# Leaving one weight tile of each light-expert chunk unsplit, as fp32, in a two-layer decoder trunk

## The chip, the cores and the metric

The kernel runs on one core of a Trainium2 chip. The metric is the device time of one launch in microseconds (us), here the median of three runs. TensorE (PE) multiplies, VectorE (DVE) and ScalarE (ACT) work on tiles in SBUF and PSUM, and SyncE (SP) issues the loads from HBM.

## The reference, cut to what matters

Two decoder layers on a sequence of 256 tokens of width 1024. Each mixes attention and a state-space scan; the first ends in a dense feed-forward block, the second in eight experts of which each token uses two. All inputs are float32. The experts are the part that the change touches:

```python
def _swiglu(h, wg, wu, wd):
    return (jax.nn.silu(h @ wg) * (h @ wu)) @ wd
...
    logits = (x2d @ w_router).astype(jnp.float32)
    top_v, top_i = lax.top_k(logits, TOP_K)
...
        return _swiglu(xb, wg[e], wu[e], wd[e]) * g[:, None]
```

Here wg and wu are 1024 x 3584 and wd is 3584 x 1024 for each of the eight experts.

## The kernel before

**Weights.** All weights come as tiles of 128 x 1024 float32 (512 KB), each by one DMA on SP's queue. An expert is worked through in 7 chunks (`NCH`) of 512 hidden columns, and a chunk has 12 tiles: 0 to 3 of the gate matrix, 4 to 7 of the up matrix, 8 to 11 of the down matrix. So an expert is 7 x 12 = 84 tiles or 44.04 MB.

**Splitting.** `load` (L510) fetches a tile `w` and hands it to `split` (L528): ACT writes a copy rounded to fp32r, `wh`, and DVE writes the rest, `wl` = `w` - `wh`, again as fp32r. PE multiplies by `wh` and `wl` in place of the float32 tile. `load` has an argument `whole` that leaves the split out and returns `(w, None)`; the mixer of the first layer uses it for its first eight weight tiles, whose matmuls stand in the trace as `bank<-w,h`.

**Heavy and light experts.** After routing, the experts are sorted by how many tokens they got. The four with most tokens are heavy: 128 rows each, activations split as well, three matmuls for each 128 x 512 piece of a weight tile (L545). The four others are light: at most 64 tokens each, the rounded activations in columns 0 to 63 of the stationary operand (`lx`, or `ht2` on the way down) and their rests in columns 64 to 127. A light expert needs only two matmuls for each piece, one by `wh` and one by `wl` (`both`, L1398); `join` (L1403) adds the lower half of the bank to the upper one. `light_up` (L1410) works tiles 0 to 7 of a chunk and writes `sg` and `ht2`, `light_down` (L1432) tiles 8 to 11. The places are taken in the order 0, 4, 1, 5, 2, 6, 3, 7 (`TURNS`), where 0 to 3 are heavy and 4 to 7 light, so a heavy expert and a light one follow each other and a light one comes last. In `moe` (L1442) the down half of a chunk is issued after the up half of the next.

**Order of the work.** Nothing is written to the engines directly. Every operation goes into a plan (`Plan.add`, L170) with its cost (`Plan.cost`, L209) and, on PE, its columns (`Plan.cols`, L204). `Plan.order` (L238) then sets one order of operations on all engines, each by the longest path that it still has before it, with corrections by stage (`BONUS`); the loads stay in the order in which the program asks for them. Tiles `w`, `wh`, `wl` and most others share 44 slots of 512 KB (`NM`), so a load can start only when a slot is free. `split` marks its ACT copy with a turn, so that splits start in the order of the loads, and with the number of `wh` that may be alive (`ks`).

Of the kernel before, what the change touches and what calls it, by code (L numbers as in the profile page):

```python
# [10 lines left out]
F32 = mybir.dt.float32  # L11
F32R = mybir.dt.float32r
# [16 lines left out]

TURNS = (0, 4, 1, 5, 2, 6, 3, 7)  # L30
GROUPS = {0: (0,), 1: (1,), 2: (2, 3), 4: LIGHT}
HEADS = [0, 4, 1, 5, 2, 6, 3, 7]
EPS = 1e-6
BIG = 1e30
# [113 lines left out]
class Plan:  # L148
# [54 lines left out]
    @staticmethod  # L203
    def cols(method, a):  # L204
        n, k = int(np.prod(a[2].shape[1:])), a[1].shape[0]
        return n * k / 128 * (2 if method == "transpose" else 1 if a[1].buf.dtype == F32R else 4)

    @staticmethod
    def cost(eng, method, a, k):  # L209
        size = lambda v: int(np.prod(v.shape[1:]))  # L210
        if method == "registers":
            return 0.5
        if eng == "DMA":
            return int(np.prod(a[0].shape)) * 4 / Plan.rate + 0.01
        n = max(size(v) for v in a if isinstance(v, View))
        if eng == "PE":
            if method == "transpose":
                return 2 * size(a[2]) / 2400 + 0.001
            if a[1].buf.dtype == F32R:
                return max(size(a[2]), 256) / 2400 + Plan.between  # L220
            return 4 * max(size(a[2]), size(a[1])) / 2400 + 0.0054
        if eng == "ACT":
            return 0.05 + n * 0.000876 + (0.06 if any(isinstance(v, View) for v in k.values()) else 0)
        if eng == "POOL":
            return max(0.35, 0.05 + n * 0.0006)
        if method in ("tensor_scalar", "tensor_copy"):
            fast = all(v.buf.kind != "ps" for v in a if isinstance(v, View))
            ptr = method == "tensor_scalar" and isinstance(a[2], View)
            return 0.066 + n * (0.00055 if fast else 0.00104) + 0.062 * ptr
        ptr = method in ("scalar_tensor_tensor", "tensor_scalar") and any(isinstance(v, View) for v in a[2:3])  # L230
        return 0.068 + n * 0.00104 + 0.062 * ptr
# [6 lines left out]
    def order(self, slots):  # L238
# [65 lines left out]
        while done < n:  # L304
# [83 lines left out]
            if e == "PE":  # L388
                if ticks.get(int(t / TICK) - 1, 0) < WARM:
                    cost *= 2  # L390
                m = int((t + cost) / TICK)
                ticks[m] = ticks.get(m, 0) + o["cols"]
# [53 lines left out]
class Kernel:  # L446
# [500 lines left out]
    def attention(self, l, prm, rs0, qb, kvb, whole):  # L947
# [63 lines left out]
        def score(gi):  # L1011
            t, h0, n = groups[gi]
            bank = self.bank()
            nk = 128 * (t + 1)
            for i in range(0, n, 2):
                self.mm3(bank[:, i * nk:(i + 2) * nk], *(x if x is None else x[:, (h0 + i) // 2, t, :] for x in qT),
                         *(x if x is None else x[:, :, 0:nk] for x in kd), True, True)
            mk = mask if t else mask[:, 128:256]
            st, pt[gi] = self.two("st")
            st = st.rearrange("p (h k) -> p h k", h=n)  # L1020
            tt(st, bank.rearrange("p (h k) -> p h k", h=n), mk.unsqueeze(1).to_broadcast([128, n, nk]), OP.add)
            c0 = 8 * t + h0
            cols = nm[:, c0:c0 + n]
            nc.vector.tensor_reduce(cols, st, AX.X, OP.max)
            stt(cols, cols, -1.0, nsink[:, h0:h0 + n], OP.mult, OP.min)
            for i in range(n):
                act(st[:, i, :], st[:, i, :], AF.Exp, bias=nm[:, c0 + i:c0 + i + 1], accum_out=den[:, c0 + i:c0 + i + 1])
            sc[gi] = st
# [369 lines left out]
    def both(self, out, x, w, first):  # L1398

        for i, b in enumerate(w):  # L1400
            self.nc.tensor.matmul(out, x, b, start=first and i == 0, stop=False, skip_group_check=True)

    def join(self, bank):  # L1403

# [5 lines left out]
    def light_up(self, src, of, rs):  # L1410
        g = []
        for q in range(2):
            bank = self.bank()
            for n in range(4):
                w = self.load(src[4 * q + n])
                for i in range(2):
                    self.both(bank, of(2 * n + i), [x[:, 512 * i:512 * i + 512] for x in w], n + i == 0)
            g.append(self.join(bank))
        h = self.H("sg")[0:ROOM]
        self.act(h, g[0], AF.Silu, scale=rs)  # L1420
        self.stt(h, g[1], rs, h, OP.mult, OP.mult)
        bank = self.bank()
        for i in range(4):
            self.nc.tensor.transpose(bank[:, ROOM * i:ROOM * i + ROOM], h[:, 128 * i:128 * i + 128], self.ident[0:ROOM, 0:ROOM])
        b = bank[:, :4 * ROOM].rearrange("p (k m) -> p k m", k=4)
        ht = self.H("ht2", F32R)
        v = ht.rearrange("p (k q m) -> p k q m", k=4, q=2)
        self.act(v[:, :, 0], b, AF.Copy)
        self.tt(v[:, :, 1], b, v[:, :, 0].bitcast(F32), OP.subtract)
        return ht  # L1430

    def light_down(self, i, src, ht, acc, then):  # L1432
        for half in range(2):
            for n in range(2):
                w = self.load(src[2 * half + n])
                for m in range(2):
                    k = 2 * n + m
                    self.both(acc[half], ht[:, 128 * k:128 * k + 128], [x[:, 512 * m:512 * m + 512] for x in w], i + k == 0)
            if then:
                then(half)  # L1440

    def moe(self, R):  # L1442
# [11 lines left out]
        for turn, j in enumerate(TURNS):  # L1454
            if j in GROUPS:
                self.plan.after = [mark] if j else []
                got = self.gather(GROUPS[j], hn) if j < HEAVY else self.gather_light(hn)
                self.plan.after = []
                for n, i in enumerate(GROUPS[j]):
                    rows[i] = (n, *got)  # L1460
# [210 lines left out]
def _lay_out(inp):  # L1671
# [4 lines left out]
    w = f(inp["w_in"])  # L1676
    q = w[:, :, :512].reshape(DEPTH, D, 8, 64)[:, :, HEADS].reshape(DEPTH, D, 512)
    kv, u = w[:, :, 512:768], w[:, :, 768:]
# [6 lines left out]

    both = lambda ms, ncol: np.stack([tiles(m, ncol) for m in ms])
    a["win_u"], a["win_q"], a["win_kv"] = both(u, 512), both(q, 512), both(kv, 256)
    a["wglu"] = both(f(inp["w_glu"]), 512)
    wo = f(inp["w_o"])
    wo = np.concatenate([wo[:, :512].reshape(DEPTH, 8, 64, D)[:, HEADS].reshape(DEPTH, 512, D), wo[:, 512:]], axis=1)  # L1690
    a["wo"] = both(wo, 512)

    def ffn(g, u, d):
# [18 lines left out]
    prm[:, :, 65] = np.tile(f(inp["k_norm_g"]), (1, 2))  # L1712
    prm[:, :, 66:74] = f(inp["sinks"])[:, None, HEADS]
    ag = f(inp["attn_out_g"]).reshape(DEPTH, 8, 64)[:, HEADS].reshape(DEPTH, 512)
    gains = [f(inp["attn_norm_g"]), np.concatenate([ag, f(inp["ssm_out_g"])], axis=1), f(inp["ffn_norm_g"])]
# [23 lines left out]
```

## Time and profile before

| | us |
|---|---|
| median of 3 runs | 1455.64 |
| lowest and highest | 1454.06 to 1456.81 |
| the profiled execution's own time | 1456.36 |
| its span | 1454.5 |
| PE matmul busy | 1395.2 (96%) |
| PE weight load busy | 1085.9 (75%) |
| DVE busy | 1239.1 (85%) |
| ACT busy | 1049.5 (72%) |
| bytes moved, mean rate | 422.59 MB, 291 GB/s |

The span is what the profile covers; the remaining 1.9 us of the profiled execution lie around it. The busy shares are means over the mixers, the dense block (up to about 480 us) and the experts (from then on), which have different limits, so the experts have to be read for themselves. All recorded operations stand at one line of a helper (L443), so they are told apart by their tiles.

### The profile page before, as it was taken

To read this page: it belongs to the slowest core of one execution; us is meant where nothing else is said; L and a number is where in the kernel's file an instruction comes from. 1 tells how busy PE (TensorE), PEld (TensorE's weight loads), DVE (VectorE), ACT (ScalarE), POOL (GpSimd) and SP (SyncE) were. 2 spreads that over 40 slices of the span, in tenths; PEclk is the share of its full clock that TensorE was granted. 3 is DMA by queue.
4 is the path that set the end of the run, shared out by engine and by line. 5 is a ranking of instruction groups with operands and counts; after the bars stand their busy time and mean duration, and the time that the engine had idled before them with its cause. 6 is when DMAs were issued, how large, how long until landed. Compare 5 with 4: busy or idle time off the path is not lost. (4 is left out here: it accounts for less than half of the span.)

```text
span 1454.5 us, 20913 instructions
## 1 busy us (share of the span) xinstructions
PE 1395.2 (96%) x6558; PEld 1085.9 (75%) x6558; DVE 1239.1 (85%) x1668; ACT 1049.5 (72%) x1350; POOL 25.4 (2%) x44
## 2 busy tenths in 40 slices
PE   7999999999999999997999998999999989999996
PEld 4888888888888777875678875668886667887564
DVE  7888885454795798998889999989999999999996
ACT  5586754445446488797787788978879878778875
POOL 3000110000000000000000000000000000000000
PEclk9999999999999999998999999989999999999998
DMA  5356155554347589599999999989999999999990
GB/s 215 106 175 230 66 167 183 189 192 173 121 171 283 199 302 348 193 395 340 348 375 380 384 400 367 393 326 362 386 383 381 348 397 390 380 384 393 387 378 33
DMA packets 116901, 422.59 MB, mean 291 GB/s; under 512 B 13360, under 2 KB 13872, under 8 KB 116784
## 3 DMA queue, kind: packets, MB, share of 16 engines
q1 hardware_dynamic: 116784, 421.20, 77.6%
q8 instruction: 53, 0.87, 0.2%
q14 instruction: 64, 0.52, 0.1%
HBM read 420.10 MB, written 1.05 MB: 290 GB/s over the span
## 5 line engine op out<-in xcount | busy, mean ns | idle before, releaser
L443 DVE TENSOR_TENSOR wl<-w,wh 128x1024 fp32r<-128x1024 f32 x786 | 917.2, 1217 | 95.1 <-ACT wh L443 48.3
L443 ACT ACTIVATE wh<-w 128x1024 fp32r<-128x1024 f32 x786 | 784.9, 1052 | 139.5 <-PE bank L443 83.8
L443 PE MATMUL bank<-wh,lx 128*128 128x512 f32 x448 | 181.6, 413 | 18.6 <-ACT sg L443 15.1
L443 PE MATMUL bank<-wl,lx 128*128 128x512 f32 x448 | 186.3, 418 | 5.6 <-DVE wl L443 5.3
L443 PE MATMUL bank<-wh,xh 128*128 128x512 f32 x448 | 174.7, 396 | 3.4 <-ACT sg L443 2.7
L443 PE MATMUL bank<-wl,xh 128*128 128x512 f32 x448 | 173.0, 395 | 1.0 <-DVE wl L443 0.9
L443 PE MATMUL bank<-wh,xl 128*128 128x512 f32 x448 | 171.8, 393 | 0.2 <-DVE xl L443 0.2
L443 PEld LDWEIGHTS bank<-wh,lx 128*128 128x128 f32 x448 | 88.3, 197 | 41.5 <-ACT sg L443 19.5
L443 PEld LDWEIGHTS bank<-wl,lx 128*128 128x128 f32 x448 | 87.6, 196 | 38.7 <-DVE wl L443 14.4
L443 PE MATMUL bank<-wl,hth 128*128 128x512 f32 x336 | 115.8, 397 | 0.0
L443 PE MATMUL bank<-wh,hth 128*128 128x512 f32 x336 | 115.7, 398 | 0.0
L443 PE MATMUL bank<-wh,htl 128*128 128x512 f32 x336 | 112.8, 394 | 0.0
L443 PEld LDWEIGHTS bank<-wh,xh 128*128 128x128 f32 x448 | 84.1, 188 | 22.6 <-ACT sg L443 3.0
L443 PEld LDWEIGHTS bank<-wl,xh 128*128 128x128 f32 x448 | 84.4, 188 | 22.2 <-DVE wl L443 4.3
L443 PEld LDWEIGHTS bank<-wh,xl 128*128 128x128 f32 x448 | 84.0, 188 | 18.1 <-DVE xl L443 1.0
L443 PE MATMUL bank<-wh,hh 128*128 128x512 f32 (+1 forms) x288 | 91.5, 385 | 0.4
L443 PE MATMUL bank<-wl,hh 128*128 128x512 f32 (+1 forms) x288 | 90.1, 381 | 0.0
L443 PE MATMUL bank<-wh,hl 128*128 128x512 f32 (+1 forms) x288 | 89.8, 380 | 0.0
L443 PE MATMUL bank<-wl,ht 128*128 128x512 f32 x224 | 84.5, 420 | 1.7 <-DVE wl L443 1.7
L443 PE MATMUL bank<-wh,ht 128*128 128x512 f32 x224 | 85.5, 425 | 0.4 <-ACT sg L443 0.3
L443 PEld LDWEIGHTS bank<-wh,hth 128*128 128x128 f32 x336 | 62.3, 188 | 13.9 <-issue 0.5
L443 PEld LDWEIGHTS bank<-wh,htl 128*128 128x128 f32 x336 | 62.9, 188 | 13.1
(306 smaller groups left out, 1685.4 us busy)
## 6 DMA issues: line engine op xcount, KB each, us to landing
w<-in_moe_dram SPq DMA_DIRECT2D x672, 512.0 KB, 6.1
w<-in_dense_dram SPq DMA_DIRECT2D x84, 512.0 KB, 4.3
w<-in_wo_dram SPq DMA_DIRECT2D x16, 512.0 KB, 4.3
w<-in_win_u_dram SPq DMA_DIRECT2D x8, 512.0 KB, 5.4
w<-in_win_q_dram SPq DMA_DIRECT2D x8, 512.0 KB, 7.5
w<-in_win_kv_dram SPq DMA_DIRECT2D x4, 512.0 KB, 3.6
w<-in_wglu_dram SPq DMA_DIRECT2D x4, 512.0 KB, 3.7
X<-in_x_dram SPq DMA_DIRECT2D x2, 512.0 KB, 5.0
```

What stands on the lines that cost most here:

```text
L443: getattr(engines[o["eng"]], o["method"])(*map(real, o["a"]), **{n: real(v) for n, v in o["k"].items()})
```

## The change

A tuple `ENTIRE = (7,)` names the tiles of a light chunk that are loaded whole: tile 7, the last of the up matrix. `both` then issues one matmul for each piece, with the stationary operand read as float32 (`bitcast`) and the raw tile as the moving one. The loop of `light_down` is written the same way, but it has tiles 8 to 11, of which none is named. The planner's cost and column rules now look at the type of the moving operand's tile (`a[2]`) where they looked at the stationary one's (`a[1]`).

```diff
+ENTIRE = (7,)
...
-        return n * k / 128 * (2 if method == "transpose" else 1 if a[1].buf.dtype == F32R else 4)
+        return n * k / 128 * (2 if method == "transpose" else 1 if a[2].buf.dtype == F32R else 4)
...
-            if a[1].buf.dtype == F32R:
+            if a[2].buf.dtype == F32R:
...
         for i, b in enumerate(w):
-            self.nc.tensor.matmul(out, x, b, start=first and i == 0, stop=False, skip_group_check=True)
+            self.nc.tensor.matmul(out, x if w[1] is not None else x.bitcast(F32), b, start=first and i == 0, stop=False, skip_group_check=True)
+            if w[1] is None:
+                break
...
-                w = self.load(src[4 * q + n])
+                w = self.load(src[4 * q + n], 4 * q + n in ENTIRE)
                 for i in range(2):
-                    self.both(bank, of(2 * n + i), [x[:, 512 * i:512 * i + 512] for x in w], n + i == 0)
+                    self.both(bank, of(2 * n + i), [x if x is None else x[:, 512 * i:512 * i + 512] for x in w], n + i == 0)
...
-                w = self.load(src[2 * half + n])
+                w = self.load(src[2 * half + n], 8 + 2 * half + n in ENTIRE)
```

The planner's rules make the rest. Up to the first gather of the experts the order of the operations is the same on every engine; from there on PE, DVE and ACT run another order, while SP's loads keep theirs.

PE, the last chunk of the last light expert, before: the end of its up half and what follows (`lx` is the activations, `ht` with a number the hidden activations of one chunk, `low,PTl` the join, `K,sg` the transposes of `sg`).

```order
L443 MATMUL bank<-wl,lx 128x512 x2
L443 MATMUL bank<-wh,lx 128x512
L443 MATMUL bank<-wl,lx 128x512
L443 MATMUL bank<-low,PTl 64x512
L443 MATMUL bank<-K,sg 128x64 x4
L443 MATMUL bank<-low,PTl 64x512
L443 MATMUL bank<-K,sg 128x64 x4
L443 MATMUL bank<-wh,ht_13283 128x512 x2
```

The down half of the last chunk but one (`ht_13283`) stood behind the last up half.

The same place with the change:

```order
L445 MATMUL bank<-wl,lx 128x512
L445 MATMUL bank<-w,lx 128x512 x2
L445 MATMUL bank<-wh,ht_13001 128x512
L445 MATMUL bank<-wl,ht_13001 128x512
L445 MATMUL bank<-wh,ht_13001 128x512
L445 MATMUL bank<-wl,ht_13001 128x512
L445 MATMUL bank<-wh,ht_13001 128x512
L445 MATMUL bank<-low,PTl 64x512
```

Two matmuls by the raw tile stand where four by `wh` and `wl` stood, and the down half of the chunk before (`ht_13001`) now begins ahead of the last join.

DVE, the end of the program, before (`X` are the adds to the result, `yl` the split of an expert's output):

```order
L443 TENSOR_TENSOR wl<-w,wh 128x1024 x8
L443 TENSOR_TENSOR ht_13091<-bank,ht_13091 128x4x64
L443 TENSOR_TENSOR wl<-w,wh 128x1024 x11
L443 SCALAR_TENSOR_TENSOR sg<-bank,rsl,sg 64x512
L443 TENSOR_TENSOR wl<-w,wh 128x1024 x2
L443 SCALAR_TENSOR_TENSOR sg<-bank,rsl,sg 64x512
L443 TENSOR_TENSOR ht_13283<-bank,ht_13283 128x4x64
L443 TENSOR_TENSOR wl<-w,wh 128x1024 x3
L443 TENSOR_TENSOR ht_13300<-bank,ht_13300 128x4x64
L443 TENSOR_TENSOR wl<-w,wh 128x1024 x3
```

and with the change:

```order
L445 TENSOR_TENSOR ht_12868<-bank,ht_12868 128x4x64
L445 TENSOR_TENSOR wl<-w,wh 128x1024 x7
L445 SCALAR_TENSOR_TENSOR sg<-bank,rsl,sg 64x512
L445 TENSOR_TENSOR wl<-w,wh 128x1024 x4
L445 TENSOR_TENSOR ht_13001<-bank,ht_13001 128x4x64
L445 TENSOR_TENSOR wl<-w,wh 128x1024 x7
L445 SCALAR_TENSOR_TENSOR sg<-bank,rsl,sg 64x512
L445 TENSOR_TENSOR wl<-w,wh 128x1024 x3
L445 TENSOR_TENSOR ht_13134<-bank,ht_13134 128x4x64
L445 TENSOR_TENSOR wl<-w,wh 128x1024 x3
```

Where the two last chunks' `sg` stood close together behind a run of 11 splits, each chunk now has its `sg` and `ht` among 11 splits of its own.

## Rows read from the trace of the kernel before

**Rows 1.** Stretches of the experts: us, busy time by engine, granted clock, DMA share, GB/s.
```profile
500.00:620.00 120.00, 118.50 (x541) 93.35 (x541) 111.67 (x118) 96.27 (x110) 0.00 (x0) 1.00 0.74 266
620.00:732.00 112.00, 102.70 (x411) 73.09 (x409) 102.24 (x108) 92.62 (x114) 0.00 (x0) 0.92 0.94 358
732.00:848.00 116.00, 116.00 (x523) 95.08 (x523) 105.81 (x99) 90.80 (x100) 0.00 (x0) 1.00 1.00 384
848.00:970.00 122.00, 111.01 (x461) 79.81 (x460) 116.50 (x126) 105.03 (x128) 0.00 (x0) 0.96 0.97 373
970.00:1086.00 116.00, 116.00 (x515) 94.85 (x516) 107.06 (x100) 90.18 (x96) 0.00 (x0) 0.98 0.98 372
1086.00:1213.00 127.00, 116.12 (x462) 83.73 (x462) 122.08 (x121) 110.49 (x128) 0.00 (x0) 0.95 0.99 379
1213.00:1316.00 103.00, 103.00 (x467) 84.26 (x467) 94.27 (x89) 81.63 (x91) 0.00 (x0) 1.00 1.00 385
1316.00:1414.00 98.00, 92.35 (x356) 62.61 (x355) 94.18 (x94) 83.43 (x98) 0.00 (x0) 0.97 1.00 386
1414.00:1448.20 34.20, 28.96 (x109) 20.54 (x108) 28.91 (x33) 22.95 (x29) 0.00 (x0) 0.90 0.15 59
```

**Rows 2.** The same view, 20 us at a time, inside light experts.
```profile
900.00:920.00 20.00, 19.46 (x71) 12.37 (x69) 19.34 (x20) 16.51 (x19) 0.00 (x0) 0.94 0.95 351
920.00:940.00 20.00, 19.56 (x81) 14.64 (x82) 20.00 (x21) 17.50 (x21) 0.00 (x0) 1.00 1.03 409
1120.00:1140.00 20.00, 16.78 (x61) 11.36 (x59) 18.59 (x22) 15.52 (x19) 0.00 (x0) 0.83 0.91 311
1380.00:1400.00 20.00, 17.65 (x72) 12.01 (x71) 20.00 (x20) 18.02 (x23) 0.00 (x0) 1.00 1.03 410
```

**Rows 3.** Timeline of the end: SP's last expert loads, then DVE.
```profile
1340.23 73.64 SPq L443 DMA_DIRECT2D w<-in_moe_dram  x55
...
1414.33 12.82 DVE L443 TENSOR_TENSOR wl<-w,wh 128x1024 fp32r<-128x1024 f32 x11
1427.07 0.74 DVE L443 SCALAR_TENSOR_TENSOR sg<-bank,rsl,sg 64x512 f32<-64x512 f32 x1
...
1435.55 3.48 DVE L443 TENSOR_TENSOR wl<-w,wh 128x1024 fp32r<-128x1024 f32 x3
```

**Rows 4.** Timeline of ACT, a run of splits at the end.
```profile
1415.56 8.64 ACT L443 ACTIVATE wh<-w 128x1024 fp32r<-128x1024 f32 x9
```

**Rows 5.** Timeline of PE: four matmuls in a row in the last light expert.
```profile
1420.60 0.39 PE L443 MATMUL bank<-wl,lx 128*128 128x512 f32 x1
1420.83 0.39 PE L443 MATMUL bank<-wh,lx 128*128 128x512 f32 x1
1421.05 0.39 PE L443 MATMUL bank<-wl,lx 128*128 128x512 f32 x1
1421.28 0.39 PE L443 MATMUL bank<-wh,lx 128*128 128x512 f32 x1
```

**Rows 6.** Matmuls by raw tiles: their timeline in the first mixer, and all of their tile.
```profile
34.09 1.88 PE L443 MATMUL bank<-w,h 128*128 128x512 f32 x4
35.81 0.38 PE L443 MATMUL bank<-K,GB 128*128 128x128 f32 x2
...
L443 PE MATMUL bank<-w,h x64: 592/592/1062, 9.8 to 45.8; 128*128 128x512 f32 x64
```

**Rows 7.** Waits of SP's queue in the second light expert, 848 to 970 us.
```profile
SPq L443 <- PE bank L443: 51.7, 48, 3.8
SPq L443 <- DVE wl L443: 22.9, 14, 6.9
```

**Rows 8.** Timeline of PE: the down halves of the two last chunks begin.
```profile
1431.61 0.69 PE L443 MATMUL bank<-K,sg 64*128 64x64 f32 x4 [1.05 <-DVE sg L443]
1432.23 1.22 PE L443 MATMUL bank<-wh,ht 128*128 128x512 f32 x2
1433.25 1.05 PE L443 MATMUL bank<-wl,ht 128*128 128x512 f32 x2
```

More of the change, by code (lines that the diff above doesn't have):

```diff
@@ L1434, in light_down @@
             for n in range(2):
-                w = self.load(src[2 * half + n])
+                w = self.load(src[2 * half + n], 8 + 2 * half + n in ENTIRE)
                 for m in range(2):
                     k = 2 * n + m
-                    self.both(acc[half], ht[:, 128 * k:128 * k + 128], [x[:, 512 * m:512 * m + 512] for x in w], i + k == 0)
+                    self.both(acc[half], ht[:, 128 * k:128 * k + 128], [x if x is None else x[:, 512 * m:512 * m + 512] for x in w], i + k == 0)
             if then:
```

## The prediction

> **What bounds the kernel now.** The change touches only light experts, so the page's shares over the whole span say little, and I read the busy time stretch by stretch first [rows 1]. I cut at the `sg` of each expert: 620 to 732, 848 to 970, 1086 to 1213 and from 1316 on are mostly the four light experts, the others heavy. In the heavy stretches from 732 on PE is busy 116.00 of 116.00, 116.00 of 116.00 and 103.00 of 103.00 us, and DVE about 92%. In the light ones it is the other way round. The second light expert has DVE busy 116.5 of 122 us, the third 122.08 of 127, the fourth 94.18 of 98: 95 to 96% each. PE shows 111 of 122 and 116 of 127, but that column is filled by overlapping matmuls; they follow each other every 0.227 us [rows 5], so the 462 of the third light expert need at most 105 of the 127 us.
>
> The loads are close behind. An expert is 44.04 MB. The light experts get 358, 373, 379 and 386 GB/s [rows 1]; in 20 us pieces the rate swings between 311 and 410 GB/s, DVE being full or nearly full all the while [rows 2]. At 386 GB/s, the best of these long stretches, an expert would take 114.1 us, at 409 GB/s 107.7. So light experts of 122 and 127 us are not at the speed of the loads. What SP's queue waits for there is a free slot: 51.7 us for PE and 22.9 us for DVE in the second light expert [rows 7], and PE frees `wh` and `wl` only after DVE has made them.
>
> The end shows it plainest. SP issues its last weight load by 1413.87 (1340.23 + 73.64), but DVE is then in a run of 11 splits, reaches the `sg` of the last chunk but one at 1427.07, and finishes its last split at 1439.03 [rows 3]. The 34 us behind the loads are a backlog of splits.
>
> **What the change removes.** One split in 12 in each of 28 light chunks.
> DVE: a split in a run takes 12.82/11 = 1.165 us [rows 3], so 28 x 1.165 = 32.6 us, or 8.2 us an expert.
> ACT: 8.64/9 = 0.96 us [rows 4], 26.9 us in all. ACT was busy 105 of 122 and 110 of 127 us there, so I cost this at nothing; DVE's load hides it.
> Slots: a split tile takes `w`, `wh` and `wl`, a raw one only `w`, though until PE has read it. A chunk asks for 34 slots in place of 36. This helps the loads; I give it no time of its own.
>
> **What it adds.** Four matmuls by fp32r pieces (4 x 0.227 = 0.91 us) become two by float32 pieces. Such matmuls run in the first mixer. Its eight whole tiles give 8 tiles x 2 pieces x 2 token blocks = 32 matmuls, and the trace has 64 records of them, so each is two records. Four records start at 34.09 and the next matmul at 35.81 [rows 6]: 0.43 us a record, 0.86 us a matmul, 1.72 us a tile. PE gains 0.81 us a tile, 5.7 us an expert, 22.7 us in all. The third light expert leaves PE 127 - 105 = 22 us, the second 122 - 461 x 0.227 = 17 us, and the 5.7 us fit. Without that cover each tile costs 0.81 us on the path. Only in the last chunk do I charge it, 0.8 us, since little is left there to cover it.
>
> The raw tile's matmul now waits for the landing itself instead of for `wl`, so it can start earlier than its predecessors did; behind it on PE stand the join and then `sg`, which had waited for that same tile before. SP's loads keep their order.
>
> **What moves.** The planner's new costs give another order from the first gather of the experts on. The first heavy expert's instructions are the same, and I take its move as zero. DVE idles 120 - 111.67 = 8.3 us in 500 to 620 [rows 1], so the move could gain up to that and I allow as much the other way. At the very end the order has the last chunk but one's down half partly ahead of the last join, where all 32 matmuls of two down halves stood behind the last transposes; 7 + 16 = 23 now stand there. Nine matmuls less are 9 x 0.227 = 2.0 us. Before, they began slowly: two start at 1432.23 and the next two at 1433.25, 0.5 us each, after PE had waited 1.05 us for `sg` [rows 8], and the granted clock averages 0.90 over the last 34 us [rows 1], so part of them ran at 1.2 instead of 2.4 GHz. I count nothing for the clock.
>
> **The sum**, by light expert.
> First (620 to 732): DVE is busy 102.2 of 112 us, so it is not the only limit; of 8.2 us I credit 2.
> Second: 8.2 us, but 122 can fall only to 114.1 by the loads at 386 GB/s: 7.9.
> Third: 8.2 us by DVE. With the heavy expert behind it the pair takes 127 + 103 = 230 us for 88.08 MB, 228.2 at 386 GB/s, which allows only 1.8. At 409 GB/s all 8.2 would come. I take 5, between them, since PE and not the loads held the heavy stretch.
> Fourth with the end: DVE holds the path to 1439, so 8.2, and 2.0 for the order, less 0.8.
> Together 2 + 7.9 + 5 + 8.2 + 2.0 - 0.8 = 24.3 us. The profiled execution took 1456.4 us, so 1432.1; the median of the runs is 0.7 below that execution: 1431.4, say 1432.
>
> The bounds. Below: all 32.6 us of DVE and the 2.0 return, with the 8.3 us of the first stretch, 42.9 less 0.8, about 1414. Above, for this case: only the second expert and the end give back, 7.9 + 8.2 - 0.8 = 15.3, about 1441.
>
> **The rivals.**
> The loads are the limit, and the swings are theirs. Then the light experts keep their length and only the backlog at the end shrinks: 8.2 less 0.8, about 1448. For it: DMA share is 0.94 to 1.00 in all light stretches. Against it: 409 and 410 GB/s in two of them while DVE was full, 311 in another [rows 2].
> The Trainium skill ("DMA: Bandwidth & Descriptors", the table at its head and the section Bandwidth) puts the HBM limit of a core at about 358 GB/s when both cores of its pair stream, and lets one core alone go higher. By the lower figure an expert would need 44.04/358 = 123 us, and this rival would hold. The trace disagrees with that figure here: 386 GB/s over 98 us [rows 1].
>
> PE becomes the limit of the light experts. Some raw tiles fall into stretches where the next heavy expert's matmuls fill PE, at least the first and the last chunk of each light expert: 8 x 0.81 = 6.5 us. If PE fills everywhere it is 22.7 us, with nothing gained elsewhere: 1462 to 1478. It decides once PE's spare time in a light chunk falls under 0.81 us; now it is 17/7 = 2.4 to 22/7 = 3.1. For it: PE is always full in the heavy stretches, and 19.56 of 20 us even in one light piece [rows 2]. Against: the spare time just worked out.
>
> The gain does not arrive. The new order costs what the splits save, as a stall at one boundary between experts: the third light expert's 127 us against the second's 122 is such a spread, and three of these, 15, with a weak gain of 15 give about 1456. That the change does not do what it says is excluded: the order has 758 splits on DVE where 786 stood, and 56 matmuls by raw tiles.
>
> **How the numbers follow.** DVE's time returns (1414 to 1441): 0.62. Loads limit, 1448: 0.18. No gain, 1453 to 1458: 0.08. PE limits, 1462 and more: 0.12. What a measurement of this kernel can tell from no change is about 0.2%, 2.9 us. So faster 0.80, same 0.07, slower 0.13, as a part of the third case ends above that bound. The range of 8 in 10 runs from 1414 to 1454: it takes in the first two and the nearer half of the third, and leaves out PE as the limit.
>
> **What would show it.** In the profile of the changed kernel: 758 splits; two records of about 0.43 us spacing for each raw matmul; the second light expert 114 to 116 us long with the load rate at 380 GB/s or more; DVE under 92% busy in the light stretches; the time from the last load issue to the end under 27 us instead of 34. If the light experts keep their lengths with DVE clearly idle, the loads or the slots were the limit. If PE waits for nothing in light stretches and they are longer, PE is. A shift in 500 to 620 us would be the planner's, not the split's.

## The result and the profile after

The changed kernel takes 1437.44 us (median of 4 runs, 1435.29 to 1439.02) against 1454.85 for the kernel before (4 runs, 1453.50 to 1456.81): ratio 0.9878, interval 0.9860 to 0.9897. That is 17.4 us less, where 24 was forecast and 1432 given as the time. The range held it. The mechanism held only in part, as the runs below show.

The light stretches of [rows 1] again, the last one up to 1400 us in place of 1414 (busy times of PE, weight load, DVE, ACT and POOL; granted clock, DMA share, GB/s):

```profile
620.00:732.00 112.00, 107.07 (x437) 74.20 (x436) 101.18 (x108) 92.31 (x115) 0.00 (x0) 0.97 0.98 362
848.00:970.00 122.00, 119.61 (x496) 83.29 (x495) 115.34 (x125) 104.19 (x129) 0.00 (x0) 1.00 0.98 371
1086.00:1213.00 127.00, 122.54 (x475) 82.69 (x474) 116.20 (x119) 99.42 (x118) 0.00 (x0) 0.97 0.99 378
1316.00:1400.00 84.00, 80.44 (x301) 49.95 (x299) 75.25 (x77) 65.96 (x78) 0.00 (x0) 1.00 1.02 401
```

Equal times no longer hold equal work, so the expert boundaries are better read from the last `sg` of each expert on DVE's timeline (`rse` stands in the heavy ones, `rsl` in the light ones). The lines at 1215.51 and 1199.13 are the first `sg` of the last heavy expert, and `cnt` is DVE's last operation of the program. Before:

```profile
622.51 0.74 DVE L443 SCALAR_TENSOR_TENSOR sg<-bank,rse,sg 128x512 f32<-128x512 f32 x1
732.26 0.74 DVE L443 SCALAR_TENSOR_TENSOR sg<-bank,rsl,sg 64x512 f32<-64x512 f32 x1 [0.82 <-PE bank L443]
848.25 0.75 DVE L443 SCALAR_TENSOR_TENSOR sg<-bank,rse,sg 128x512 f32<-128x512 f32 x1
969.92 0.74 DVE L443 SCALAR_TENSOR_TENSOR sg<-bank,rsl,sg 64x512 f32<-64x512 f32 x1 [1.20 <-PE bank L443]
1086.30 0.74 DVE L443 SCALAR_TENSOR_TENSOR sg<-bank,rse,sg 128x512 f32<-128x512 f32 x1
1212.90 0.74 DVE L443 SCALAR_TENSOR_TENSOR sg<-bank,rsl,sg 64x512 f32<-64x512 f32 x1 [0.54 <-PE bank L443]
1215.51 0.75 DVE L443 SCALAR_TENSOR_TENSOR sg<-bank,rse,sg 128x512 f32<-128x512 f32 x1 [0.73 <-PE bank L443]
1316.08 0.75 DVE L443 SCALAR_TENSOR_TENSOR sg<-bank,rse,sg 128x512 f32<-128x512 f32 x1 [0.73 <-PE bank L443]
1430.81 0.75 DVE L443 SCALAR_TENSOR_TENSOR sg<-bank,rsl,sg 64x512 f32<-64x512 f32 x1 [0.74 <-ACT sg L443]
1448.00 0.14 DVE L1546 CAST cnt<-most 128x1 int32<-128x1 f32 x1
```

and after:

```profile
620.75 0.75 DVE L445 SCALAR_TENSOR_TENSOR sg<-bank,rse,sg 128x512 f32<-128x512 f32 x1
723.43 0.74 DVE L445 SCALAR_TENSOR_TENSOR sg<-bank,rsl,sg 64x512 f32<-64x512 f32 x1 [5.13 <-PE bank L445]
839.18 0.75 DVE L445 SCALAR_TENSOR_TENSOR sg<-bank,rse,sg 128x512 f32<-128x512 f32 x1 [0.44 <-PE bank L445]
952.97 0.73 DVE L445 SCALAR_TENSOR_TENSOR sg<-bank,rsl,sg 64x512 f32<-64x512 f32 x1
1066.74 0.75 DVE L445 SCALAR_TENSOR_TENSOR sg<-bank,rse,sg 128x512 f32<-128x512 f32 x1 [1.53 <-ACT sg L445]
1185.15 0.74 DVE L445 SCALAR_TENSOR_TENSOR sg<-bank,rsl,sg 64x512 f32<-64x512 f32 x1
1199.13 0.75 DVE L445 SCALAR_TENSOR_TENSOR sg<-bank,rse,sg 128x512 f32<-128x512 f32 x1 [0.43 <-PE bank L445]
1299.39 0.75 DVE L445 SCALAR_TENSOR_TENSOR sg<-bank,rse,sg 128x512 f32<-128x512 f32 x1 [0.28 <-PE bank L445]
1415.58 0.74 DVE L445 SCALAR_TENSOR_TENSOR sg<-bank,rsl,sg 64x512 f32<-64x512 f32 x1 [1.51 <-PE bank L445]
```

A light expert and the heavy one behind it take 225.7 us before and 218.4 after (first pair), 238.1 and 227.6 (second), 229.8 and 232.7 (third); the fourth light expert takes 114.7 and 116.2. So the gain sits in the first two pairs, 7.3 and 10.5 us, and the third pair and the last light expert lose 2.9 and 1.5 of it.

Taken by their own last `sg`, the first three light experts get 7.1, 7.9 and 8.2 us shorter (109.8, 121.7 and 126.6 us before; 102.7, 113.8 and 118.4 after), close to the 8.2 us of DVE that left each. But the heavy expert behind the third then takes 114.2 us where it took 103.2. Before, its first `sg` came 2.6 us behind the last one of the light expert, after, 14.0: the two had been interleaved more closely. So where one expert ends depends on the order, and the pairs are the safer measure.

Of the signs that the prediction named, the splits are 758, the second light expert takes 113.8 us (forecast 114 to 116) at 379 GB/s (380 or more), and the end behind the last load is shorter, as shown below. But DVE is not under 92% busy in this expert: it has 107.71 of 113.79 us, 95%.

```profile
839.18:952.97 113.79, 111.40 (x461) 77.16 (x459) 107.71 (x116) 99.39 (x123) 0.00 (x0) 1.00 0.99 379
```

The order that was planned for the new work is kept by the chip: this is DVE's timeline over the last chunks, where [rows 3] shows a run of 11 splits before.

```profile
1388.29 4.62 DVE L445 TENSOR_TENSOR wl<-w,wh 128x1024 fp32r<-128x1024 f32 x4
1393.63 1.23 DVE L445 TENSOR_TENSOR wl<-w,wh 128x1024 fp32r<-128x1024 f32 x1 [0.72 <-ACT wh L445]
1395.29 2.36 DVE L445 TENSOR_TENSOR wl<-w,wh 128x1024 fp32r<-128x1024 f32 x2 [0.43 <-ACT wh L445]
1399.16 0.74 DVE L445 SCALAR_TENSOR_TENSOR sg<-bank,rsl,sg 64x512 f32<-64x512 f32 x1 [1.52 <-PE bank L445]
...
1411.70 2.36 DVE L445 TENSOR_TENSOR wl<-w,wh 128x1024 fp32r<-128x1024 f32 x2 [0.43 <-ACT wh L445]
1415.58 0.74 DVE L445 SCALAR_TENSOR_TENSOR sg<-bank,rsl,sg 64x512 f32<-64x512 f32 x1 [1.51 <-PE bank L445]
```

SP's row shows the last weight load issued by 1404.81 (1299.96 + 104.85), 9.1 us earlier than before, and the program ends about 25 us behind it instead of 34:

```profile
1299.96 104.85 SPq L445 DMA_DIRECT2D w<-in_moe_dram  x80
...
1429.80 0.14 DVE L1550 CAST cnt<-most 128x1 int32<-128x1 f32 x1
```

But the last chunk has a period of 16.42 us (1415.58 - 1399.16), and the seven chunks of this light expert take 16.6 us each on average where they took 16.4 before. In each of the last two DVE waits about 0.7 + 0.43 us for ACT and 1.5 us for PE. It is no longer DVE that is full here: DVE stands in a chain. PE's and ACT's timelines around one raw tile show the links:

```profile
1411.89 0.40 PE L445 MATMUL bank<-wl,lx 128*128 128x512 f32 x1
1412.13 1.88 PE L445 MATMUL bank<-w,lx 128*128 128x512 f32 x4
1413.44 0.80 PE L445 MATMUL bank<-wh,ht 128*128 128x512 f32 x1
1414.04 0.59 ACT L445 ACTIVATE low<-bank 64x512 fp32r<-64x512 f32 x1 [1.43 <-PE bank L445]
1414.08 0.39 PE L445 MATMUL bank<-wl,ht 128*128 128x512 f32 x1
...
1415.09 0.45 PE L445 MATMUL bank<-low,PTl 64*64 64x512 f32 x1
```

The raw tile's four records hold PE from 1412.13 for about 1.7 us, as reckoned from [rows 6]: the second matmul behind them starts 1.95 us later, at 1414.08, and 0.23 us of that are the first one, shown from 1413.44. ACT meanwhile waits 1.43 us: `low` is next in its queue, and the splits `wh` behind it wait with it. Then come `low`, the join and `sg`. The chain of work that ended last goes through the same place:

```profile
1405.97 2.35 PE bank L445 x8
...
1408.95 1.07 ACT wh L445
1410.05 1.24 DVE wl L445
1411.33 4.23 PE bank L445 x13
...
1416.25 1.22 DVE wl L445
```

The raw tile's four records are among the 13 of PE, and the `wh` of the chain stands on ACT right behind a `low`.

### The profile page after: what moved, and what is told of

The parts are those of the page before. It is cut to its first block, busy times and chain, and to the rows that moved or that the text cites. A ratio compares the mean times of both kernels' runs of the same rounds, so it can differ in the third digit from the quotient of the medians.

```text
span 1436.0 us, 20731 instructions
## 1 busy us (share of the span) xinstructions
PE 1399.2 (97%) x6558; PEld 1070.7 (75%) x6558; DVE 1204.7 (84%) x1640; ACT 1013.6 (71%) x1322; POOL 25.4 (2%) x44
## 3 DMA queue, kind: packets, MB, share of 16 engines
HBM read 420.10 MB, written 1.05 MB: 293 GB/s over the span
## 4 chain that ended last, share of the span: by engine, by line
PE 88%; DVE 5%; DMA 2%; issue 2%; ACT 1%; SPq 0%; DVEq 0%; ACTq 0%
PE bank L445 88%; DVE wl L445 3%; DMA w<-in_moe_dram 2%; DVE X L445 1%; DMA w<-in_win_u_dram 1%; ACT wh L445 1%; ACT st L445 0%; SPq L445 0%; DVE ht L445 0%; DVE htl L445 0%; ACT xh L445 0%; DVE psm L445 0%; DVE xl L445 0%; DVE yl L445 0%; ACT sg L445 0%
## 5 line engine op out<-in xcount | busy, mean ns | idle before, releaser
L445 DVE TENSOR_TENSOR wl<-w,wh 128x1024 fp32r<-128x1024 f32 x758 | 884.3, 1219 | 90.9 <-ACT wh L445 59.2
L445 ACT ACTIVATE wh<-w 128x1024 fp32r<-128x1024 f32 x758 | 749.7, 1051 | 81.8 <-PE bank L445 32.2
L445 PE MATMUL bank<-wl,lx 128*128 128x512 f32 x392 | 161.3, 416 | 6.1 <-DVE wl L445 5.8
L445 PE MATMUL bank<-wh,lx 128*128 128x512 f32 x392 | 155.0, 406 | 7.7 <-DVE ht L445 4.5
L445 PEld LDWEIGHTS bank<-wl,lx 128*128 128x128 f32 x392 | 75.2, 192 | 42.2 <-DVE wl L445 20.2
L445 PEld LDWEIGHTS bank<-wh,lx 128*128 128x128 f32 x392 | 75.3, 192 | 24.8 <-ACT wh L445 4.1
L445 PE MATMUL bank<-wh,ht 128*128 128x512 f32 x224 | 88.4, 432 | 0.6 <-DVE ht L445 0.6
L445 ACT ACTIVATE low<-bank 64x512 fp32r<-64x512 f32 x64 | 37.9, 594 | 52.4 <-PE bank L445 51.6
```

Source lines behind the costliest of these rows:

```text
L445: getattr(engines[o["eng"]], o["method"])(*map(real, o["a"]), **{n: real(v) for n, v in o["k"].items()})
```

## The experiments

Theory A is the prediction's: DVE's time came back, PE's price is covered, the order hardly counts. Theory B: the planner's new order does it. Theory C, formed after the first eight runs: a light chunk is a chain through queues that keep their order, in which every engine's time counts, and the order decides how much of it overlaps. Ratios are to the kernel before, run beside them; 0.9878 is the change itself. Differences between runs that were not made side by side are differences of these ratios times 1455 us.

**The raw tile without a new plan.** The plan of the kernel before, from which the split is then left out:

```diff
+                if whole:
+                    ops[-2]["drop"] = ops[-1]["drop"] = True
+                    plain = ops[-2]["a"][1]
...
+                    if whole:
+                        ops[-1]["drop"] = True
+                        ops[-2]["a"] = (bank, x.bitcast(F32), plain[:, 512 * i:512 * i + 512])
```

> The raw tile in the engines' order of the kernel before: the plan is made as if tile 7 were still split, and only then are its split left out and its four matmuls replaced by two float32 ones. Theory A (the splits that are gone from DVE give the gain, whatever the order): 1436 to 1443 us, most of the 17 us. Theory B (the planner's new order gives it): 1451 us or more. In between: both have a part, in proportion.

Measured 1460.55 us against 1456.76, ratio 1.0034 (1.0017 to 1.0050): slightly slower than before. 32.6 us of DVE and 26.9 of ACT went, 22.7 of PE came, and nothing returned. Theory A in its plain form falls here. ACT's `low` now waits for PE more than twice as long as in the kernel before, where the whole program has 24.1 us (shown below):

```profile
ACT low L446 <- PE bank L446: 56.9, 46, 4.6
```

**The planner's rules alone.**

```diff
-        return n * k / 128 * (2 if method == "transpose" else 1 if a[1].buf.dtype == F32R else 4)
+        return n * k / 128 * (2 if method == "transpose" else 1 if a[2].buf.dtype == F32R else 4)
...
-            if a[1].buf.dtype == F32R:
+            if a[2].buf.dtype == F32R:
```

> The kernel before with the planner's two new rules alone and no raw tile: the same instructions in another order from the first gather of the experts on. Theory A: within 4 us of the kernel before, 1451 to 1459. Theory B: 1437 to 1445.

1444.77 us, ratio 0.9929 (0.9904 to 0.9954): about 10 us come without any raw tile, so theory B has a part. The largest cost that these rules change there is that of the first gather (`PP,X`, 16 matmuls), each of which the planner now takes for 0.12 us instead of 0.22. With that and a few smaller prices another order comes out. In the first light expert DVE is then busy 110 of 112 us, where [rows 1] had 102, and the loads run at 385 instead of 358 GB/s:

```profile
620.00:732.00 112.00, 105.42 (x453) 75.68 (x452) 110.07 (x118) 100.12 (x123) 0.00 (x0) 0.98 1.00 385
```

**The raw tile with the old rules.** The planner believes that its matmul is about four times as fast as it is; the two lines of the diff above are turned round in the changed kernel.

> The changed kernel with the planner's old rules, so that it orders the raw tiles' matmuls as if one took a quarter of its time. Theory A: within 5 us of the changed kernel, 1432 to 1443, as the same work is left out. Theory B: the knowledge of the true cost matters, 1447 or more.

1463.12 us, ratio 1.0050 (1.0031 to 1.0068): the same operations as the changed kernel, 1.7% slower. With the raw tile priced wrongly the gain turns into a loss.

**The raw tile with both prices right.** The rule asks for both operands, so the gather is costed as in the kernel before and the raw tile as in the change:

```diff
-            if a[2].buf.dtype == F32R:
+            if a[1].buf.dtype == a[2].buf.dtype == F32R:
```

> The changed kernel with a rule that asks for both operands: the raw tile's matmul is costed at four passes, as in the change, and the first gather's too, as before (the change makes the planner take that gather for one pass). If the true cost of the raw tile is what the planner needed: 1432 to 1442. If the planner's order merely happens to be better with the wrong gather: 1450 or more.

1439.07 us, ratio 0.9893 (0.9871 to 0.9915), no different from the change. So the gather's wrong price, which gave 10 us by itself, is not needed once the raw tile is there, and the two gains do not add. What the change needed of its rules was the price of the raw tile: 0.9893 against 1.0050, with the reserve that each of these is one order among many.

The waits of the whole program show where the wrongly priced order loses: ACT's `low` waits for PE (us in total, times, longest) in the kernel before

```profile
ACT low L443 <- PE bank L443: 24.1, 23, 6.4
```

in the wrongly priced order

```profile
ACT low L445 <- PE bank L445: 83.3, 51, 5.2
```

in the order with both prices right

```profile
ACT low L445 <- PE bank L445: 56.7, 45, 3.6
```

and in the changed kernel

```profile
ACT low L445 <- PE bank L445: 51.6, 41, 4.7
```

Of the waits for the raw tiles' own matmuls `low` has, in the wrongly priced order and in the one with both prices right,

```profile
  ACT low L445: 42.6, 24
  ACT low L445: 18.8, 17
```

This fits a planner that thinks the raw tile short, and so puts `low` early into ACT's queue, where the splits then stand behind it.

**DVE's time back, order unchanged.** The added operation has no cost in the plan and is taken up first, so that everything else keeps its place:

```diff
+                if w[1] is None:
+                    tag, self.plan.tag = self.plan.tag, "extra"
+                    self.nc.vector.tensor_reduce(self.S(1, "at"), w[0], AX.X, OP.max)
+                    self.plan.tag = tag
```

> The changed kernel, order and slots unchanged, but DVE reads each raw tile once in a reduction of 128x1024 whose result nobody uses (about 1.15 us in place of the 1.165 us of the split that went). Theory A (DVE's time is what came back): 1450 to 1458, the gain is gone. If ACT's time or the slots gave it: 1435 to 1441.

1452.36 us, ratio 0.9977 (0.9961 to 0.9993): 14 us slower than the change for some 32 us on DVE (one reduction takes 1.21 us in the profile, a lone split 1.23). Nearly the whole gain goes, so in the new order DVE's time is what the change lives on, as theory A has it. But less than half of it counts, and theory B is not refuted: PE's added 22.7 us are still in this run.

**ACT's time back, order unchanged.** As above with

```diff
+                    self.act(w[0], w[0], AF.Copy)
```

> The changed kernel, order unchanged, but ACT copies each raw tile onto itself (1.05 us, the time of the copy that went), and the matmul waits for that. Theory A (DVE alone): within 4 us of the changed kernel, 1434 to 1441. If ACT's time has a part: 1445 or more.

1443.89 us, ratio 0.9926 (0.9900 to 0.9951): 7 us slower than the change for 28 x 1.05 = 29 us on ACT. Theory A had nothing here, 1445 was the rival's figure; it is between them and nearer to the rival. ACT's time was not free, though a part of the 7 us can lie in the edit: the raw tile's matmul now waits for the copy, where it waited only for the landing (3.6 us of such waits in the profile).

**PE's price doubled.**

```diff
+            for again in range(2 if o.get("twice") else 1):
```

> The changed kernel with each raw tile's two float32 matmuls issued twice (so these tiles' products are added twice): PE gains another 28 x 1.72 = 48 us. If PE's spare time in the light experts covers it, as I reckoned 2.4 to 3.1 us a chunk before and 0.8 less now: up to 10 us slower, 1437 to 1447. If PE is the limit there: 1470 to 1485.

1482.34 us, ratio 1.0196 (1.0164 to 1.0228): 46 us slower than the change for 48 us on PE. There is next to no cover. ACT's `low` waits for PE longer in the whole program:

```profile
ACT low L446 <- PE bank L446: 97.6, 51, 5.3
```

and DVE and the loads do less in the same stretch (848 to 970 us: DVE 105.59 busy against 115.34 in the change, loads at 346 GB/s against 371):

```profile
848.00:970.00 122.00, 120.19 (x479) 81.65 (x478) 105.59 (x113) 96.66 (x118) 0.00 (x0) 1.00 0.94 346
```

**PE's price halved.**

```diff
                     self.both(bank, of(2 * n + i), [x if x is None else x[:, 512 * i:512 * i + 512] for x in w], n + i == 0)
+                    if raw and i:
+                        self.plan.ops[-1]["drop"] = True
```

> The changed kernel, order unchanged, with only the first of each raw tile's two float32 matmuls (so half of tile 7's product is left out): PE loses 28 x 0.86 = 24 us and is where it was with four fp32r matmuls. Theory C (a light chunk is a chain through the in-order queues: DVE's last split, PE's raw tile, ACT's low, the join, sg; each link counts in full): 1413 to 1422. Theory A' (PE's price was covered, as I predicted, and doubling it only went past the cover): 1434 to 1440.

1422.30 us, ratio 0.9772 (0.9744 to 0.9800): 15 us faster than the change for 24 us off PE. So the longer float32 matmuls cost the change some 15 us of what the missing splits earn. That is the step of the prediction that was most wrong.

**DVE's and ACT's time back and PE's halved**, in the changed kernel's order: the three edits above together.

> The changed kernel, order unchanged, with DVE's and ACT's time for each raw tile given back (a reduction and a copy that nobody needs) and one of the two float32 matmuls left out (so half of tile 7's product is missing): the engines' times of the kernel before, in the new order. If the new order gives the gain: 1437 to 1446, as with the rules alone. If the work that went gives it: 1452 or more.

1478.00 us, ratio 1.0158 (1.0133 to 1.0182): far slower than both sides had it, 56 us above the run with PE's price halved for 32 + 29 = 61 us of DVE and ACT. But these are not the dependences of the kernel before. The copy overwrites the tile that the reduction reads, so ACT waits for DVE, and the matmul waits for the copy; in a split it is DVE that waits for ACT. For the reductions alone ACT waits 38.1 us, a wait that neither kernel has:

```profile
ACT w L447 <- DVE at L447: 38.1, 21, 5.8
```

So this run does not tell what the new order is worth with the old amounts of work, and theory B stays open. An estimate from the single runs: DVE's 14 and ACT's 7 less PE's 15 make 6 us of the change's 18 (0.9878), which leaves some 12 for the order, about what the rules alone bring. It takes for granted that these answers add up, which no run shows.

**No loads for the raw tiles.**

```diff
+                if 4 * q + n in ENTIRE:
+                    w = (plain, None)
+                else:
+                    w = self.load(src[4 * q + n])
+                    plain = self.plan.ops[-2]["a"][1]
```

> The changed kernel without the loads of tile 7 of the light chunks; its matmuls read the raw tile 6 instead (so the product of tile 7 is wrong data). 28 x 512 KB = 14.7 MB less, 38 us at 386 GB/s; DVE, ACT and PE keep their work. If the loads are the limit of the changed kernel: 1400 to 1418. If they are not: 1433 to 1439.

1436.96 us, ratio 0.9871 (0.9838 to 0.9903): nothing changes with 14.7 MB less to load. In the stretch of the second light expert the loads now run at 350 GB/s, DMA share 0.94, and the program takes the same time. One reserve: the planner makes another order for this run on PE, DVE and ACT, so it is not the change with its loads alone taken away.

```profile
848.00:970.00 122.00, 117.87 (x482) 82.87 (x481) 111.60 (x117) 102.62 (x125) 0.00 (x0) 0.97 0.94 350
```

In the changed kernel itself no wait of an engine is put down to an expert's load, while the same list has one for the dense block:

```profile
ACT wh L445 <- DMA w<-in_dense_dram: 29.1, 20, 3.9
```

So the loads do not hold the experts as a whole. They are not quite out of it: the chain that ended last passes through five landings, 25.9 us together, four of them in the last light expert. The prediction's floor of 386 GB/s was none, as the 401 GB/s over 84 us in the first block above show.

**Two raw tiles.**

```diff
-ENTIRE = (7,)
+ENTIRE = (3, 7)
```

> Two raw tiles in each light chunk, 3 and 7: DVE loses another 32.6 us, PE gains another 22.7. If DVE is still the limit of the light experts, another 10 to 17 us go: 1420 to 1428. If the loads hold them by now, 1433 to 1439, and only the backlog behind the last load gets shorter. If PE has become the limit, 1441 or more.

1443.51 us, ratio 0.9913 (0.9891 to 0.9936): the second raw tile brings no gain, and the ratio stands a little above that with one, the ends of the intervals overlapping. Together with the halved price this suggests that PE's 22.7 us for it cost as much as its splits save; the order is another one here too.

**Another raw tile.**

```diff
-ENTIRE = (7,)
+ENTIRE = (5,)
```

> The changed kernel with tile 5 raw in place of tile 7. Theory C: the 1.72 us of PE no longer stand between DVE's last split and the join, so sg waits less, 0.5 to 1.2 us a chunk: 1405 to 1425, unless the planner's new order takes it back. Theory A' (only the amount of work counts): within 5 us of the changed kernel, 1433 to 1442.

1439.64 us, ratio 0.9904 (0.9882 to 0.9926): no better. As theory C has it, `low` no longer waits behind the raw tile: of the operations that waited for matmuls by raw tiles, `ACT low` stood first in the changed kernel,

```profile
  ACT low L445: 20.2, 18
```

and is missing with tile 5. But `low` as a whole waits for PE longer than in the change,

```profile
ACT low L445 <- PE bank L445: 66.5, 37, 8.2
```

so the wait moved to other matmuls. Theory C had the place of the wait right, and the gain from moving the raw tile wrong.

## Why the prediction was right or wrong

**What bounds the light experts.** I read DVE's 95 to 96% as the limit. Half right: given back to DVE, 32 us cost 14. But removing them in the old order, with PE's 22.7 us added, gave nothing (1.0034). An engine that is 95% busy in a chain of queues need not be the limit by itself. No run takes DVE's time out of the old order without adding PE's.

**The removed work.** DVE's 8.2 us an expert was the right amount and not the right worth, about 0.45 us of each microsecond. ACT I costed at nothing; 29 us given back cost 7.

**The added work.** The price was right: the raw records in the change have a median of 592 ns as in [rows 6], and the four hold PE about 1.7 us. "The 5.7 us fit" was wrong. The spare time was a sum over the stretch, 17 to 22 us, and there was none at the place where the raw tile stands, ahead of `low`, the join and `sg`. PE's time counts at 15 of 24 us downwards and 46 of 48 upwards.

**What moves.** I gave the order 2.0 us. It was worth 23 us between the raw tile priced wrongly and rightly (1.0050 and 0.9893), and 10 without any raw tile. Set beside the old work in that last order, the raw tile is worth 7 us (0.9878 against 0.9929), not 17. That the planner's rule belongs to the change as much as the raw tile does was visible in the diff, and I took it for bookkeeping. The first stretch, which I bounded by 8.3 us, moved by 1.8.

**The sum.** By place it measured 7.3 for the first light expert and the heavy one behind it (forecast 2), 10.5 for the second pair (7.9), -2.9 for the third (5) and, from 1316.08 and 1299.39 to the `cnt` at the end (1448.00 before, 1429.80 after), 1.5 for the fourth and the end (9.4), besides 1.8 ahead of them: 18.2 in the profiles. That it came near 24 is luck: errors of both signs met. PE's price, of which I charged 0.8, costs about 15, ACT's time, which I left out, brings up to 7, and DVE's time, put at 8.2 us an expert, brings about 14 in all. So the forecast gave some 22 us to the work and 2 to the order, where the estimate above has 6 and 12.

**The rivals.** The loads as the limit are not borne out: the run without them takes the same time, and the waits name none. The Trainium skill's figure of about 358 GB/s ("DMA: Bandwidth & Descriptors", section Bandwidth) is for a core whose pair streams as well. This kernel runs on one core, and the figure is passed again here: 401 GB/s over 84 us in the first block above. PE as the limit was nearest to the truth in its mechanism, though not in its sign, and its point of decision, spare time summed over a chunk, was the wrong test. That the new order could turn the gain into a loss, the third rival, is what the wrong price shows, by 6 us.

**What stays open.** Which of the moved operations gives the rules alone their 10 us; why the third pair got longer; what the new order is worth with the old work in it; and how much of each run with another plan is the planner's chance. The gather's 1.6 us in the plan and a few smaller prices moved the old work by 10, so the chance can be large. The three plans with one raw tile and its true price (0.9878, 0.9893 and 0.9904) agree within 4 us, which speaks for a smaller one there but does not exclude it.

## What to carry to other kernels

Where a planner or a person has fixed the order on queues that keep it, work that is taken away may come back only if the order is made again with its true costs: here the change gave 17 us with the raw tile's price in the plan and lost 4 to 6 without. A new order can also move the time by itself, here by 10 us, so it needs a run of its own with the old work. Spare time of an engine covers added work only at the place where that work stands; before counting on it, look at who waits next in line, here ACT's `low` and the splits behind it. A work balance of several engines at 85 to 100% is tested by giving time back to each with the order held, without new waits between them, and the answers need not add up.

## What the runs showed of the hardware

The mean granted clock rose from 0.976 to 0.989 over the span, and in the light stretches from 0.92, 0.96 and 0.95 [rows 1] to 0.97, 1.00 and 0.97, a mixture of 1.2 and 2.4 GHz that holds more of the latter. I had counted nothing for it. The raw tile's long matmuls may leave PE fewer pauses, but no run separates this from the order: the rules alone have 0.984 over the span, the raw tile priced wrongly 0.982, both prices right 0.995.
